# Matmul operands padded to lie alike mod 256 bytes, x loaded in quarters, and ten early pairs in a hybrid attention and MLP block

## The chip, the cores and the metric

The kernel runs on one core of a Trainium2 chip. The metric is the device time of one execution in microseconds (us). The time before is the median of three runs, 1524.86 us (1524.47 to 1524.96). A measurement of this kernel can tell a difference of about 0.2%, some 3 us, from no change.

Engines are named as in the profile: PE is TensorE's matmul, PEld its weight load, DVE is VectorE, ACT is ScalarE, POOL is GpSimd, SP is SyncE, which issues the DMAs.

## What is computed

One decoder layer on 1024 tokens of width 1024, in float32:

```python
h = rmsnorm(x, g_mix)
proj = h @ w_in            # q, k, v of three branches, an indexer, 3 gate groups
o_swa = sliding_window_attention(...)      # window 128, sinks
o_dsa = dsa_attention(...)                 # indexer scores, top 256 keys
o_mem = memory_cross_attention(...)        # 256 memory tokens
gates = sigmoid(gate_logits + b_gate)
merged = g0 * (o_swa @ w_proj_swa) + g1 * (o_dsa @ w_proj_dsa) + g2 * (o_mem @ w_proj_mem)
x = x + merged @ w_out
h = rmsnorm(x, g_mlp)
hid = square(relu(h @ w_mlp_in))           # 1024 x 4096
x = x + hid @ w_mlp_out
return rmsnorm(x, g_final)
```

## The kernel before, in words

Every large product is made of three matmuls of fp32r parts: each operand is split into a high part (a rounded copy, by ACT, line 93) and a low part (the rest, a subtraction on DVE or POOL), and `mm3` (lines 146 to 149) issues high x high, high x low and low x high into one PSUM bank. A matmul has a moving operand of up to 512 columns and a stationary operand of 128 columns, which a weight load brings in first. In a row of the profile the moving operand and the stationary one stand behind the arrow.

The stages, in the order of time:

- **Attention** (to 613 us). x is normalised and transposed, the indexer scores are computed, VectorE and ScalarE search the top 256 keys bit by bit (lines 535 to 575), and the three attention branches run. The gate products (`gt_g`, 24 units of 48 matmuls of 512 columns) have a low priority and fill PE between them.
- **Projections and merge** (613 to 745 us), with the gates read back from DRAM, then the **output projection** (`out_part`, line 908; tiles `mb_o`). It runs over `tg` (token halves) and `n` (column halves), and in each over `kp` (four pieces of w_out, 512 KB each, `raw_wo`). Each piece feeds 24 matmuls. Its result is added to x (line 982), which is loaded by eight DMAs of 512 KB (line 938) into the buffer `x2`. That buffer held `part` until then, so the DMAs wait for the last reader of `part` (line 905), and every DMA that stands behind them on SP's queue waits too.
- **Normalisation for the MLP** (to 890 us). Each token tile is scaled, transposed (`tb_h`, line 1003) and split. For the second token half the seven-product scheme of Strassen and Winograd needs sums of blocks (`T1` to `T4`, lines 1016 to 1024). While that runs, PE has the **early pairs**: for the first EARLY of 16 column pairs the two products that need the first token half alone (`mb_ep`, `mb_eq`, lines 1036 to 1047; 24 matmuls a pair). Their sum is squared behind a relu on DVE (line 1044), and both are written to DRAM.
- **MLP up** (`up_pair`, lines 1083 to 1119; 890 to 1158 us). A pair costs five products of 12 matmuls, and two more if it is not an early one. Weights are added on POOL (`load_pair`, lines 1073 to 1076) and split on ACT and DVE (`up_unit`).
- **MLP down** (`mb_dn`, lines 1135 to 1194; from 1158 us) and the final norm.

The order of the instructions on each engine is set ahead of time by a scheduler, by the priorities of `band`. Where a tile lies in SBUF is set by the pools: `base` at the bottom, `A2` above it (later `X2`, `C` and `X3` in its place), and from the other end `bigA` with the transposed activations (`hT`, `oT`, `h2T`), `A`, `G` and later `M` and `E`. The weights of most stages lie in `base` (`load_unit`, lines 112 to 122) or in `X3`. In the MLP's up stage `up_unit` goes round four slots, two in `base`, one in `X3`, one in `M`:

```python
i = ring["n"] % 4
(pool, tag, bufs) = ((base, "st", 2), (base, "st", 2), (X3, "w3", 1), (M, "u4", 1))[i]
```

## Time and profile before

| what | value |
|---|---|
| median of three runs | 1524.86 us |
| the profiled execution's own time | 1524.89 us |
| its span, first to last instruction | 1523.2 us |
| PE busy | 1454.0 us (95%) |
| DVE, ACT, POOL busy | 991.5, 638.5, 562.2 us |
| mean granted TensorE clock | 0.988 |
| DMA, mean | 106 GB/s |
| chain that ended last: PE, DVE | 71%, 17% |

The span is 1.7 us shorter than the execution's own time; what lies around it stays. Matmuls are pipelined: a row's duration holds the time in the pipeline too, and what a matmul costs in a dense stretch is the distance from its start to the next one's start. The idle time that stands before a row is the engine's own, and the arrow names what ended it.

### The profile page before, as it was taken

Reading aid. Unit: us, or ns where it says so; the run is one execution under the profiler, and the core shown is the slowest. Engines: PE = TensorE matmul, PEld = TensorE weight load, DVE = VectorE, ACT = ScalarE, POOL = GpSimd, SP = SyncE. Lnnn points to the kernel's source line nnn. Section 1 sums busy time; section 2 is a strip of 40 time slices with the busy share of each in tenths; the row PEclk is TensorE's granted clock in tenths of the full one; section 3 lists DMA queues with packets and bytes.
Section 4 is the critical chain, followed back from the end, with each engine's and each line's share of the span. In section 5 each row is a group of like instructions: output and inputs, shape, how many; then the busy total and the mean of one; then the engine's idle time right before and its main releaser. Section 6 shows DMA issues by size and latency. Waiting matters only on the chain.

```text
span 1523.2 us, 19743 instructions
## 1 busy us (share of the span) xinstructions
PE 1454.0 (95%) x7010; PEld 1215.7 (80%) x7010; DVE 991.5 (65%) x1909; ACT 638.5 (42%) x1251; POOL 562.2 (37%) x468
## 2 busy tenths in 40 slices
PE   6999999998899999999899989999998999999997
PEld 5888877897788988788678768888886888888886
DVE  7667999999986665757543966565555533444436
ACT  5545767875465444645345522222223220122213
POOL 4332224326567433445244753432223321222302
PEclk9999999999999999999999999999999999999999
DMA  6212331212112133546532444433326413323002
GB/s 215 84 56 84 104 90 58 74 46 69 50 35 70 42 100 102 158 129 215 195 131 89 146 139 142 152 127 115 101 96 230 155 59 111 111 111 111 28 14 97
DMA packets 133015, 161.51 MB, mean 106 GB/s; under 512 B 11284, under 2 KB 97332, under 8 KB 129844
## 3 DMA queue, kind: packets, MB, share of 16 engines
q1 hardware_dynamic: 132916, 160.25, 32.2%
q8 instruction: 55, 0.90, 0.3%
q14 instruction: 44, 0.36, 0.1%
HBM read 120.38 MB, written 39.85 MB: 105 GB/s over the span
## 4 chain that ended last, share of the span: by engine, by line
PE 71%; DVE 17%; issue 4%; DMA 3%; ACT 2%; POOL 1%; SPq 1%; DVEq 0%; ACTq 0%; POOLq 0%
PE mb_dn L148 7%; PE mb_dn L149 7%; PE mb_dn L147 7%; PE mb_u L147 5%; PE mb_u L148 5%; PE mb_u L149 5%; PE mb_o L919 4%; PE gt_g L148 4%; PE gt_g L147 4%; PE gt_g L149 4%; DVE tk_jk L538 3%; PE gt_p L148 1%; PE gt_p L147 1%; PE gt_p L149 1%; PE tb_u L148 1%
## 5 line engine op out<-in xcount | busy, mean ns | idle before, releaser
L148 PE MATMUL mb_dn<-wlo,hhi 128*128 128x512 f32 (+1 forms) x516 | 200.1, 388 | 1.2 <-POOL wlo L969 1.1
L147 PE MATMUL mb_dn<-whi,hhi 128*128 128x512 f32 (+1 forms) x516 | 197.9, 388 | 3.5 <-ACT whi L93 2.4
L149 PE MATMUL mb_dn<-whi,hlo 128*128 128x512 f32 (+1 forms) x516 | 200.0, 388 | 1.1 <-DVE hlo L969 1.1
L1168 DVE TENSOR_TENSOR x<-x,mb_dn 128x512 f32<-128x512 f32 x129 | 87.0, 681 | 167.8 <-PE mb_dn L149 166.9
L969 POOL TENSOR_TENSOR wlo<-wr,whi 128x1024 fp32r<-128x1024 f32 x32 | 84.9, 2670 | 225.4 <-ACT whi L93 220.2
L147 PE MATMUL gt_g<-hT_hi,hi_g 128*128 128x512 f32 x384 | 153.6, 400 | 2.0 <-DVE gs L825 1.6
L148 PE MATMUL gt_g<-hT_lo,hi_g 128*128 128x512 f32 x384 | 153.9, 401 | 0.0
L149 PE MATMUL gt_g<-hT_hi,lo_g 128*128 128x512 f32 x384 | 153.5, 400 | 0.0
L147 PEld LDWEIGHTS mb_dn<-whi,hhi 128*128 128x128 f32 x516 | 96.8, 188 | 24.1 <-ACT whi L93 2.8
L148 PEld LDWEIGHTS mb_dn<-wlo,hhi 128*128 128x128 f32 x516 | 96.9, 188 | 21.9 <-POOL wlo L969 2.1
L149 PEld LDWEIGHTS mb_dn<-whi,hlo 128*128 128x128 f32 x516 | 96.9, 188 | 21.1 <-DVE hlo L969 1.6
L93 ACT ACTIVATE hi_s<-r 128x1024 fp32r<-128x1024 f32 (+1 forms) x48 | 43.5, 916 | 165.0 <-PE mb_u L148 66.4
L93 ACT ACTIVATE hhi<-hr 128x1024 fp32r<-128x1024 f32 x32 | 32.7, 1048 | 180.8 <-PE mb_dn L148 158.6
L538 DVE TENSOR_SCALAR_CACHE_REDUCE tk_jk<-isc,tk_c 128x384 bf16<-128x384 f32 (+3 forms) x128 | 103.5, 808 | 2.5
L106 POOL TENSOR_TENSOR lo_g<-raw_g,hi_g 128x1024 fp32r<-128x1024 f32 x24 | 58.3, 2428 | 97.1 <-ACT hi_g L93 76.1
L147 PEld LDWEIGHTS gt_g<-hT_hi,hi_g 128*128 128x128 f32 x384 | 72.7, 189 | 18.2 <-DVE gs L825 2.0
L535 ACT ACTIVATE tk_jk<-isc,tk_c 128x1024 bf16<-128x1024 f32 x64 | 73.6, 1149 | 29.0 <-DVE tk_c L547 26.2
L149 PEld LDWEIGHTS gt_g<-hT_hi,lo_g 128*128 128x128 f32 x384 | 72.8, 189 | 14.8
L148 PEld LDWEIGHTS gt_g<-hT_lo,hi_g 128*128 128x128 f32 x384 | 72.6, 189 | 14.8
L147 PE MATMUL mb_u<-T_hi,hi_s 128*128 128x512 f32 x192 | 76.7, 399 | 7.0 <-ACT hi_s L93 7.0
L1073 POOL TENSOR_TENSOR r<-r,r 128x512 f32<-128x512 f32 x16 | 20.9, 1304 | 159.6 <-DMA r<-in_w_mlp_in_dram 159.6
L148 PE MATMUL mb_u<-T_lo,hi_s 128*128 128x512 f32 x192 | 76.8, 400 | 0.0
(452 smaller groups left out, 3907.5 us busy)
## 6 DMA issues: line engine op xcount, KB each, us to landing
wr<-in_w_mlp_out_dram SPq DMA_DIRECT2D x32, 512.0 KB, 3.5
hr<-hid_d SPq DMA_DIRECT2D x16, 1024.0 KB, 6.1
raw_g<-in_w_in_dram SPq DMA_DIRECT2D x24, 512.0 KB, 3.9
g_d<-gs SPq DMA_DIRECT2D x48, 256.0 KB, 2.0
gl<-g_d SPq DMA_DIRECT2D x48, 256.0 KB, 3.5
raw_wo<-in_w_out_dram SPq DMA_DIRECT2D x16, 512.0 KB, 3.5
r<-in_w_mlp_in_dram SPq DMA_DIRECT2D x16, 512.0 KB, 4.3
r<-in_w_mlp_in_dram SPq DMA_DIRECT2D x32, 256.0 KB, 2.9
```

Of the source, the lines that this page charges most:

```text
L93: nc.scalar.activation(o, i, AF.Copy)
L106: lo_engine.tensor_tensor(lo, raw, hi.bitcast(F32), op=ALU.subtract)
L147: nc.tensor.matmul(ps, st_hi, mv_hi, start=first, stop=False)
L148: nc.tensor.matmul(ps, st_hi, mv_lo, start=False, stop=False)
L149: nc.tensor.matmul(ps, st_lo, mv_hi, start=False, stop=last)
L535: nc.scalar.activation(jk[:, :n], isc[t], AF.Sign, bias=cand_f[:, j:j + 1], scale=-1.0, accum_out=cnt[:, j:j + 1])
L538: nc.vector.tensor_scalar(jk[:, :n], isc[t], cand_f[:, j:j + 1], 0.0, op0=ALU.is_ge, op1=ALU.add, accum_out=cnt[:, j:j + 1])
L919: nc.tensor.matmul(banks[i], st, (hi, hi, lo)[part_][:, kk_], start=(k == 0 and part_ == 0), stop=(k == KT - 1 and part_ == 2))
L969: engine.tensor_tensor(lo, raw, hi.bitcast(F32), op=ALU.subtract)
L1073: add(r2[:, lo4], r3[:, lo4], r2[:, hi4])
L1168: nc.vector.tensor_tensor(x2[:, t, cs], x2[:, t, cs], ps, op=ALU.add)
```

## The change

Four things. **Padding**: a pad of 96 bytes is put into `base` and one of 64 bytes into `A2`, `split_load` rounds the last dimension of its tiles up to 64 elements, and some small tiles are moved or resized, so that tiles start elsewhere. **x in quarters**: `load_x` loads 4 tiles of 512 columns (four DMAs of 256 KB) for one (tg, n) at a time. **EARLY** goes from 8 to 10. **Early stage**: the relu and square of an early pair go from one DVE operation to two ACT operations, and the low parts of the early pairs' weights and of `T3` go from POOL to DVE.

```diff
--- before.py
+++ after.py
@@ -34,7 +34,7 @@
 NEG_BIG = -float(2.0 ** 117)
 POS_BIG = float(2.0 ** 117)
 DSA_AHEAD = 2
-EARLY = 8
+EARLY = 10
 MERGE_WITH = (range(4), range(4, 6), range(6, 8), ())
 GATE_ORDER = [*range(8), *range(16, 24), *range(8, 16)]
 GATES_EARLY = 10
@@ -86,6 +86,9 @@
     p1_d = [dram.tile([P, 512], F32, name=f"p1_d{i}") for i in range(EARLY)]
 
     base = ctx.enter_context(tc.tile_pool(name="base", bufs=1))
+
+
+    base.tile([P, 24], F32, name="pad")
     ident_r = base.tile([P, P], F32R, name="ident")
     ident = ident_r.bitcast(F32)
 
@@ -98,7 +101,8 @@
         return hi, lo
 
     def split_load(slots, shape, srcs, nm, lo_engine):
-        raw, hi, lo = (pool.tile(list(shape), dt, tag=tag, name=f"{part}_{nm}", bufs=bufs)
+        pitch = list(shape[:-1]) + [-(-shape[-1] // 64) * 64]
+        raw, hi, lo = (pool.tile(pitch, dt, tag=tag, name=f"{part}_{nm}", bufs=bufs)[..., :shape[-1]]
                        for (pool, tag, bufs), dt, part in zip(slots, (F32, F32R, F32R), ("raw", "hi", "lo")))
         for (sl, src) in srcs:
             nc.sync.dma_start(raw if sl is None else raw[sl], src)
@@ -227,6 +231,7 @@
             chunk.append((hi, lo))
         return chunk
 
+    A2.tile([P, 16], F32, name="pad2")
     ident_f = A2.tile([P, P], F32, tag="rl", name="ident_f", bufs=2)
     make_identity(nc, ident_f)
     act_copy(ident_r, ident_f)
@@ -249,7 +254,7 @@
     sink8 = A2.tile([P, 8], F32, name="sink8")
     nc.sync.dma_start(sink8, sinks[0].partition_broadcast(P))
     nc.vector.tensor_scalar(sink8, sink8, 8.0, None, op0=ALU.mult)
-    invf = A2.tile([P, 32], F32, name="invf")
+    invf = A.tile([P, 32], F32, tag="o_sb", name="invf", bufs=2)
     nc.sync.dma_start(invf, inv_freq.partition_broadcast(P))
     pos_i = p_tile([P, P], "pos_i", I32)[:NT]
     nc.sync.dma_start(pos_i, positions[0].rearrange("(t p) -> t p", p=P))
@@ -262,8 +267,8 @@
     nc.tensor.transpose(tpc[:, 32:56], bg_r, ident[:24, :24])
     pos = A2.tile([P, NT], F32, name="pos")
     nc.vector.tensor_copy(pos, tpc[:, 0:NT])
-    bgate = A.tile([P, 24], F32, name="bgate")
-    nc.vector.tensor_copy(bgate, tpc[:, 32:56])
+    bgate = A.tile([P, 32], F32, name="bgate")
+    nc.vector.tensor_copy(bgate[:, :24], tpc[:, 32:56])
 
 
     cur_ok = A2.tile([P, P], I32, name="cur_ok")
@@ -557,8 +562,8 @@
             eqb = A2.tile([P, S], BF16, tag="rl", name=f"{gn}_eq{t}", bufs=2)[:, :n]
             cum = A2.tile([P, S], F32, tag="cum", name=f"{gn}_cum{t}")[:, :n]
             if on_act:
-                mn = A2.tile([P, 1], F32, tag="tk_mn", name=f"{gn}_mn{t}", bufs=2)
-                up = A2.tile([P, 1], I32, tag="tk_up", name=f"{gn}_up{t}", bufs=2)
+                mn = A2.tile([P, 1], F32, tag="tk_mn", name=f"{gn}_mn{t}")
+                up = A2.tile([P, 1], I32, tag="tk_up", name=f"{gn}_up{t}")
                 nc.vector.tensor_scalar(le, isc[t], T, 0.0, op0=ALU.is_le, op1=ALU.add, accum_out=c1)
                 nc.vector.scalar_tensor_tensor(cum, le, F32_MAX, isc[t], op0=ALU.mult, op1=ALU.add)
                 nc.gpsimd.affine_select(out=cum[:, t * P:], in_=cum[:, t * P:], pattern=[[-1, n - t * P]],
@@ -922,20 +927,25 @@
 
     for d in range(KT):
         merge_unit(0, d)
+
+    def load_x(tg, n):
+        with band("w"):
+            for t in range(4 * tg, 4 * tg + 4):
+                nc.sync.dma_start(x2[:, t, n * 512:(n + 1) * 512], x[t * P:(t + 1) * P, n * 512:(n + 1) * 512])
+
     first_banks = [mb_bank(f"o00{i}") for i in range(4)]
     for kp in range(KT // 2):
         out_part(0, 0, first_banks, kp)
         for d in MERGE_WITH[kp]:
             merge_unit(1, d)
+        if kp == 2:
+            x2 = X2.tile([P, NT, D], F32, tag="x2", name="x2")
+            load_x(0, 0)
 
     ctxC.close()
     X3 = ctx.enter_context(tc.tile_pool(name="X3", bufs=1, reuse_waits="tile"))
     late["pool"], late["n"] = X3, 0
 
-    x2 = X2.tile([P, NT, D], F32, tag="x2", name="x2")
-    with band("w"):
-        for t in range(NT):
-            nc.sync.dma_start(x2[:, t], x[t * P:(t + 1) * P, :])
 
 
 
@@ -970,11 +980,13 @@
 
     ctxM = ExitStack()
     for tg in range(2):
-        ss = X3.tile([P, 2, 4], F32, tag="n_ss4", name=f"ss2_{tg}", bufs=2)
+        ss = X3.tile([P, 2, 16], F32, tag="n_ss4", name=f"ss2_{tg}", bufs=2)[:, :, :4]
         for n in range(2):
             cs = slice(n * 512, (n + 1) * 512)
             banks = [mb_bank(f"o{tg}{n}{i}") for i in range(4)] if tg or n else first_banks
             for kp in range(KT // 2 if tg or n else 0):
+                if kp == 2:
+                    load_x(tg, n)
                 out_part(tg, n, banks, kp)
             with band("crit"):
                 for i in range(4):
@@ -1020,7 +1032,7 @@
                     nc.vector.scalar_tensor_tensor(lo, tps[1], -1.0, hi.bitcast(F32), op0=ALU.mult, op1=ALU.subtract)
                     nc.vector.scalar_tensor_tensor(t3, tps[1], -1.0, t3, op0=ALU.mult, op1=ALU.add)
                     nc.vector.tensor_tensor(t4, t4, t2, op=ALU.subtract)
-                    for dst, src, e in ((T2, t2, nc.vector), (T3, t3, nc.gpsimd), (T4, t4, nc.gpsimd), (T1, t1, nc.vector)):
+                    for dst, src, e in ((T2, t2, nc.vector), (T3, t3, nc.vector), (T4, t4, nc.gpsimd), (T1, t1, nc.vector)):
                         split(*(v[:, :, ts] for v in dst), src, e)
 
     def product(ps, w, mv):
@@ -1034,14 +1046,15 @@
 
 
     for c in range(EARLY):
-        a11, a12 = halves(load_unit(wcol[2 * c], f"wi{2 * c}", nc.gpsimd))
+        a11, a12 = halves(load_unit(wcol[2 * c], f"wi{2 * c}", nc.vector))
         ps1, ps2 = mb_bank(f"ep{c}"), mb_bank(f"eq{c}")
         st = M.tile([P, 2, 512], F32, tag=("stg", "u4_lo")[c % 2], name=f"st{c}")
         product(ps1, a11, B11)
         act_copy(st[:, 0], ps1)
         product(ps2, a12, B21)
         nc.vector.tensor_tensor(st[:, 1], ps2, st[:, 0], op=ALU.add)
-        nc.vector.scalar_tensor_tensor(st[:, 1], st[:, 1], 0.0, st[:, 1], op0=ALU.max, op1=ALU.mult)
+        nc.scalar.activation(st[:, 1], st[:, 1], AF.Relu)
+        nc.scalar.activation(st[:, 1], st[:, 1], AF.Square)
         with band("w"):
             nc.sync.dma_start(p1_d[c], st[:, 0])
             nc.sync.dma_start(hid_d[c][:, 0], st[:, 1])
```

Byte address, mod 256, at which a matmul's moving and stationary operand start, in the built programs (matmuls of 512 columns, unless another width is given):

| products | matmuls | before: moving, stationary | changed |
|---|---|---|---|
| gates `gt_g` | 1152 | 224, 128 | 224, 224 |
| projections `gt_p`, `mm_p`, `mb_p`, `tb_p` | 384 | 224, 128 | 224, 224 |
| memory queries `mm_mq` | 96 | 224, 64 | 224, 224 |
| output projection `mb_o` | 384 | 128 or 192, 224 | 224, 224 |
| early pairs `mb_ep`, `mb_eq` | 192 (240 in the changed one) | 224, 128 or 192 | 224, 224 |
| MLP up, weights in `base` or `X3` | 720 | 224, 128 or 192 | 224, 224 |
| MLP up, weights in `M` | 432 | 224, 224 | 224, 224 |
| MLP down `mb_dn` | 1524 | 224, 224 | 224, 224 |
| attention scores `sc_` | most | 32, 32 | 32, 32 |
| projections of 384 columns (`mm_s`, `mm_dp`) | 576 | 64, 224 | 224, 224 |

So 2928 matmuls of 512 columns lie unlike before and alike in the changed kernel (1152 + 384 + 96 + 384 + 192 + 720). Transposes and the products with the probabilities stay unlike.

Up to the output projection the order on every engine is the same in both programs. The first place where it moves is SP's queue at the load of x (`x` is the tile x2, `raw_wo` a piece of w_out). Before:

```order
L104 DMA raw_wo_8099<-in_w_out_dram 128x2x512
L938 DMA x_8067<-in_x_dram 128x1024 x8
L104 DMA raw_wo_8129<-in_w_out_dram 128x2x512
L104 DMA raw_wo_8159<-in_w_out_dram 128x2x512
L958 DMA g_mlp_t<-in_g_mlp_dram 128x1024
L104 DMA raw_wo_8189<-in_w_out_dram 128x2x512
```

Changed:

```order
L108 DMA raw_wo_8099<-in_w_out_dram 128x2x512
L934 DMA x_8037<-in_x_dram 128x512 x4
L108 DMA raw_wo_8129<-in_w_out_dram 128x2x512
L934 DMA x_8037<-in_x_dram 128x512 x4
L108 DMA raw_wo_8163<-in_w_out_dram 128x2x512
L934 DMA x_8037<-in_x_dram 128x512 x7
L108 DMA raw_wo_8193<-in_w_out_dram 128x2x512
L934 DMA x_8037<-in_x_dram 128x512
```

One piece of w_out stood behind 4 MB of x and now stands behind 1 MB of it; the later ones have 1 MB, 1.75 MB and 0.25 MB more of x ahead of them.

The second place is POOL during the normalisation (`xn` a token tile, `lo_wi` the low part of an early pair's weights, `T_lo` the low part of T3 or T4, `r_0` the first weights of the up stage). Before:

```order
L965 TENSOR_TENSOR xn_8659<-xn_8659,g_mlp_t 128x512
L106 TENSOR_TENSOR lo_wi_8862<-raw_wi_8860,hi_wi_8861 128x1024
L106 TENSOR_TENSOR lo_wi_8900<-raw_wi_8898,hi_wi_8899 128x1024
L969 TENSOR_TENSOR T_lo<-xn_8630,T_hi 128x4x128
L106 TENSOR_TENSOR lo_wi_8938<-raw_wi_8936,hi_wi_8937 128x1024
L969 TENSOR_TENSOR T_lo<-braw_8079,T_hi 128x4x128
L965 TENSOR_TENSOR xn_8688<-xn_8688,g_mlp_t 128x512
L106 TENSOR_TENSOR lo_wi_8976<-raw_wi_8974,hi_wi_8975 128x1024
```

Changed:

```order
L975 TENSOR_TENSOR xn_8671<-xn_8671,g_mlp_t 128x512
L979 TENSOR_TENSOR T_lo<-braw_8079,T_hi 128x4x128
L975 TENSOR_TENSOR xn_8700<-xn_8700,g_mlp_t 128x512
L979 TENSOR_TENSOR T_lo<-braw_8079,T_hi 128x4x128
L975 TENSOR_TENSOR xn_8729<-xn_8729,g_mlp_t 128x512
L979 TENSOR_TENSOR T_lo<-braw_8079,T_hi 128x4x128
L1086 TENSOR_TENSOR r_0_9150<-r_0_9151,r_0_9150 128x512
```

All ten `lo_wi` and the four low parts of T3 are gone from POOL.

The third place is DVE at the end of the normalisation, up to the first result of the up stage (`st` the products of an early pair, `lo_s` the low part of the up stage's first weights). Before:

```order
L969 TENSOR_TENSOR h2T_lo<-braw_8078,h2T_hi 128x4x128
L1022 TENSOR_TENSOR braw_8079<-braw_8079,xn_8717 128x4x128
L1043 TENSOR_TENSOR st_8982<-mb_eq_8981,st_8982 128x512
L969 TENSOR_TENSOR T_lo<-xn_8717,T_hi 128x4x128
L1044 SCALAR_TENSOR_TENSOR st_8982<-st_8982 128x512
L1043 TENSOR_TENSOR st_9020<-mb_eq_9019,st_9020 128x512
L1044 SCALAR_TENSOR_TENSOR st_9020<-st_9020 128x512
L969 TENSOR_TENSOR lo_s_0_9062<-r_0_9051,hi_s_0_9061 128x1024
```

Changed:

```order
L1055 TENSOR_TENSOR st_9000<-mb_eq_8999,st_9000 128x512
L1034 TENSOR_TENSOR braw_8079<-braw_8079,xn_8729 128x4x128
L110 TENSOR_TENSOR lo_wi_9111<-raw_wi_9109,hi_wi_9110 128x1024
L979 TENSOR_TENSOR h2T_lo<-braw_8078,h2T_hi 128x4x128
L979 TENSOR_TENSOR T_lo<-xn_8729,T_hi 128x4x128 x2
L1055 TENSOR_TENSOR st_9039<-mb_eq_9038,st_9039 128x512
L979 TENSOR_TENSOR lo_s_0_9160<-r_0_9149,hi_s_0_9159 128x1024
L1055 TENSOR_TENSOR st_9078<-mb_eq_9077,st_9078 128x512
L979 TENSOR_TENSOR lo_s_0_9168<-r_0_9151,hi_s_0_9167 128x512
L1055 TENSOR_TENSOR st_9117<-mb_eq_9116,st_9117 128x512
```

The squares (L1044) are gone from DVE, and two more sums of early pairs stand among the low parts of the up stage's weights. On PE, 39 matmuls of early pairs stood between the last transpose of a token tile and the first product of the up stage; now 81 do.

## Rows read from the trace of the kernel before

**Rows 1.** Windows by stage: us, busy of each engine (instructions), PEclk, DMA share, GB/s.

```profile
141.00:415.00 274.00, 260.14 (x1387) 223.14 (x1386) 265.95 (x676) 189.84 (x432) 105.86 (x118) 0.99 0.24 70
...
745.00:831.00 86.00, 77.77 (x341) 62.36 (x340) 32.49 (x48) 36.99 (x66) 32.05 (x16) 0.94 0.43 147
831.00:890.00 59.00, 49.31 (x225) 39.19 (x225) 51.97 (x64) 28.85 (x47) 41.29 (x22) 0.97 0.47 143
890.00:1158.00 268.00, 268.00 (x1153) 217.27 (x1152) 155.99 (x198) 57.45 (x66) 86.03 (x62) 0.99 0.37 124
```

**Rows 2.** Waits of PE over the span: us in total, times, longest.

```profile
PE mb_o L919 <- ACT hi_wo L93: 9.1, 2, 8.2
PE mb_u L147 <- ACT hi_s L93: 7.0, 1, 7.0
```

**Rows 3.** Timeline of PE, first matmuls of successive products of 12: pair 6, pair 7.

```profile
980.00 0.39 PE L147 MATMUL mb_u<-T_hi,hi_s 128*128 128x512 f32 x1
...
982.80 0.39 PE L147 MATMUL tb_u<-h2T_hi,hi_s 128*128 128x512 f32 x1
...
993.96 0.39 PE L147 MATMUL mb_u<-T_hi,hi_s 128*128 128x512 f32 x1
...
996.68 0.39 PE L147 MATMUL tb_u<-h2T_hi,hi_s 128*128 128x512 f32 x1
```

**Rows 4.** PE groups by form: count, busy us, mean ns, idle before.

```profile
L147 PE MATMUL mb_dn<-whi,hhi 128*128 128x512 f32 x508 | 195.6, 390 | 3.5 <-ACT whi L93 2.4 <-DVE hid L1113 1.1
L147 PE MATMUL gt_g<-hT_hi,hi_g 128*128 128x512 f32 x384 | 153.6, 400 | 2.0 <-DVE gs L825 1.6 <-ACT gs L823 0.4
L355 PE MATMUL sc_Sd<-kT_d,qT_dp 128*128 128x512 f32 x24 | 9.8, 410 | 0.0
```

**Rows 5.** Window 141 to 415, instructions on the gates' tile alone (columns as above, without POOL).

```profile
141.00:415.00 274.00, 134.78 (x536) 100.10 (x535) 9.66 (x13) 6.77 (x10) 0.99 0.24 70
```

**Rows 6.** Timeline of SP (start, us, line), then of PE.

```profile
747.40 3.78 SPq L938 DMA_DIRECT2D x<-in_x_dram  x8
751.29 1.44 SPq L104 DMA_DIRECT2D raw_wo<-in_w_out_dram  x2
...
763.17 0.80 PE L919 MATMUL mb_o<-hi_wo,mg_hi 128*128 128x512 f32 x1 [8.23 <-ACT hi_wo L93]
...
767.58 0.40 PE L919 MATMUL mb_o<-hi_wo,mg_hi 128*128 128x512 f32 x1
```

**Rows 7.** Chain of waits through that stall: start, us, what.

```profile
751.29 10.69 DMA raw_wo<-in_w_out_dram
...
762.06 1.06 ACT hi_wo L93
```

**Rows 8.** Groups of DVE, POOL and ACT in 831 to 889; low parts on DVE (ns, min/median/max).

```profile
L1044 DVE SCALAR_TENSOR_TENSOR st<-st 128x512 f32<-128x512 f32 x8 | 13.0, 1627 | 0.1
...
L969 DVE TENSOR_TENSOR T_lo<-xn,T_hi 128x512 fp32r<-128x512 f32 x4 | 5.4, 1355 | 0.0
...
L106 POOL TENSOR_TENSOR lo_wi<-raw_wi,hi_wi 128x1024 fp32r<-128x1024 f32 x6 | 15.3, 2551 | 6.1 <-ACT hi_wi L93 6.1
...
L93 ACT ACTIVATE T_hi<-xn 128x512 fp32r<-128x512 f32 x8 | 5.0, 628 | 2.8 <-DVE xn L1019 1.9 <-DVE xn L1021 0.8
...
L106 DVE TENSOR_TENSOR lo_wo<-raw_wo,hi_wo x8: 1216/1226/2295, 704.0 to 769.0; 128x1024 fp32r<-128x1024 f32 x8
```

**Rows 9.** Chain of waits into the up stage: start, us, what.

```profile
887.80 1.07 ACT hi_s L93
...
888.91 0.79 PE mb_u L147
889.70 0.43 PE mb_u L148
...
893.97 0.24 PE mb_u L149
```

**Rows 10.** Timeline of PE, the last transposes of the normalisation.

```profile
872.12 0.63 PE L1003 MATMUL tb_h<-ident,xn 128*128 128x128 f32 x4 [1.13 <-DVE xn L1021]
```

## The prediction
> **What bounds the kernel now.** I read the windows by stage first, since the engines' shares over the span mix stages with different limits. They show PE as the bound nearly everywhere: in the MLP's up stage for 268.00 of 268 us [rows 1]. Three stretches differ. From 141 to 415 us VectorE is busy for 265.95 of 274 us and PE waits for it. From 745 to 831 PE is busy for 77.77 of 86 us, and from 831 to 890 for 49.31 of 59 [rows 1]. The waits of PE put names to the last two: 9.1 us for a piece of w_out, one of them 8.2 us, and 7.0 us for the first weights of the up stage [rows 2]. So there is time to win in two ways: in the cost of a matmul where PE is full, and in the two holes.
>
> **The padding.** In a dense stretch a matmul costs the distance between starts. The timeline of the up stage has the same work from two places. The third product of pair 6 takes its weights from `base`, where the stationary operand starts at 128 and the moving one at 224: 12 matmuls from 980.00 to 982.80, 233 ns each. The third product of pair 7 takes them from `M`, where both start at 224: 12 matmuls from 993.96 to 996.68, 227 ns each [rows 3]. The difference is 6.6 ns (2.80 less 2.72 us, over 12). The mean durations go the same way: 400 ns for the gates, which lie unlike, 390 ns for the MLP's down stage, which lies alike [rows 4]. What the rows cannot part is the address from the place: `M` and the down stage's pool are at the end of SBUF that `base` is not. I take the address as the cause, because the change moves no pool and its padding is then worth the whole difference; the other reading is a rival.
>
> 2928 matmuls go from unlike to alike. Of these, those that lie under VectorE's stretch win nothing, since the end of that stretch is VectorE's: 536 gate matmuls [rows 5] and the 96 memory queries, 632 in all. The 192 of the early pairs I count below. That leaves 2104 matmuls by 6.6 ns, **13.9 us**. The bounds are nothing (the place is the cause) and 18.1 us (2736 matmuls, where VectorE's stretch shortens too). I stay at the measured difference without the covered ones. The 576 matmuls of 384 columns have no row of the same width in both layouts that is as dense; I set them at nothing, with at most 6.6 ns each, 3.8 us, as the other bound.
>
> The trace speaks against a rule here. The Trainium skill (SBUF — State Buffer, section Who interferes with whom) gives PE two read ports of SBUF, one for the moving operand and one for the weight load, independent of each other, and says that PE never waits on anyone. By it the two addresses could not matter, this term would be zero, and the sum below 15 us smaller. The trace has a difference between two equal products [rows 3], so it does not agree, unless the place makes it.
>
> The other edits of this part (a wider pitch, small tiles moved, one buffer for two in the select) add no operation and leave the order on all engines as it was up to the output projection. The buffer that is gone makes a tile's minimum wait for the tile before it, and both stand in order on VectorE anyway. I set them at nothing.
>
> **x in quarters.** SP issues x at 747.40, when the last reader of `part` is done, and the piece of w_out that PE needs next at 751.29, behind 4 MB [rows 6]. It takes 10.69 us to land, then ACT splits it in 1.06 us and PE starts at 763.17, after 8.23 us of nothing [rows 6, 7]. The idle costs more than itself: the next ten matmuls, to 767.58, stand 0.44 us apart [rows 6], against 0.23 [rows 3]: after the idle time the granted clock is at the lower of its two levels, 1.2 GHz, and it is 0.94 over the stage [rows 1]. Ten by 0.21 is 2.1 us. In the changed order 1 MB stands ahead of that piece. 4.5 MB took from 747.40 to the landing at 761.98, 14.6 us, or some 320 bytes per ns with the latency in it; so 1.5 MB take about 5 us, the piece lands near 752.5, and with ACT's 1.06 us PE could have it at about 753.5. PE ran dry at 754.94. The stall goes. What is late next are the pieces behind: the one after the batch of seven has 5.25 MB ahead of and including itself, 17 us, so it is there at 764.4 and split at 765.5; PE wants it two pieces of 24 matmuls after 754.9, at 765.8. That is close, and I set 1.5 us against the gain. The term is 8.2 + 2.1 - 1.5 = **8.8 us**, with bounds of 4 (a second hole of 5 us, below) and 10.3.
>
> **The early stage.** PE's hole of 7.0 us before the up stage [rows 2] ends with a chain from POOL's sums through ACT's split to PE at 888.91 [rows 9]. From there to 893.97 the chain has eleven matmuls, all but the first 0.43 us apart [rows 9]: 5.06 us in place of 2.6, of which I put 2.3 down to the lower clock and the rest to the first one's way through the pipeline. The two added pairs put 48 matmuls, 11 us of PE's work, into the normalisation, and take the same 48 out of the up stage. So PE's sum is unchanged, and the hole is filled where the chain is not later: 81 matmuls, 18.4 us, now follow the last transpose, where the whole way from the last transposes, at 872.12 [rows 10], to the up stage's first product took 16.8 us. I take both, 9.3 us.
>
> This holds only if the others keep pace. VectorE was busy for 51.97 of 59 us [rows 1]. It loses eight squares, 13.0 us, and gains eight low parts of weights inside the stretch, at 1.23 us each by the rows for the same shape on VectorE, 9.8 us; four low parts of T3, half as large and so set at half of that, 2.5 us; and two sums of the same size, 1.2 us [rows 8]. That is 0.5 us more. The dear end is 2.3 us for a low part (its longest row) and 1.36 for one of T3, 25 us with the sums, 12 more than the squares [rows 8]. I take the cheap end, because the operations that got dear stood beside POOL's, and POOL loses 15.3 us of `lo_wi` in the stretch and four operations of T3 [rows 8]. ACT gains two operations a pair; the nearest row is a split of the same size, 0.63 us [rows 8], so 20 of them are 12.6 us on 28.85 of 59: covered, and if ACT were the bound the cost would be a few us at most. The added DMAs (two weights of 512 KB, two stores and loads) meet a queue that is busy for 0.47 of the time [rows 1]; PE's work hides them. The 192 old early matmuls win 1.3 us by the padding, and I give 0.5 back for waits that stay. The term is 9.3 + 1.3 - 0.5 = **10.1 us**, with bounds of nothing and 13.
>
> **The sum.** 13.9 + 8.8 + 10.1 = 32.8 us, off the profiled execution's own time of 1524.89 us, which is the median within 0.03 us: **1492 us**.
>
> **Rivals.**
> - *The place, not the address, sets a matmul's cost.* The padding is worth nothing and the other terms stay: 1492 + 13.9 + 1.3 = 1507 us. For it: the fast products [rows 3, 4] have their weights at one end of SBUF. Against it: the attention scores, with both operands at that end, are no faster than the gates (410 against 400 ns, [rows 4]). The rule on PE's ports in the Trainium skill (SBUF — State Buffer) would give the same time. 8%.
> - *VectorE becomes the bound of the early stage.* At the dear end it has 64 us of work where PE has 240 matmuls, 54.5 us at 227 ns, and the transposes, and its in-order queue holds the low parts that PE waits for. The stall before the up stage stays in another form, and the term falls to nothing: 1502 us. For it: VectorE is the fullest engine after PE there. Against it: the sum of its work hardly changes at the cheap end. 10%.
> - *The batch of seven makes a new hole.* If 256 KB pieces move more slowly than the 512 KB ones, the piece behind it comes 5 us late, with up to 2 us of lower clock: 1498 us. 12%.
> - *Slower: alike operands collide.* The alike rows of the scores are 10 ns longer than the unlike ones of the gates [rows 4]; if that is what likeness does, and the pools at the far end are fast for another reason, the 2296 matmuls (2104 and 192) cost 10 ns more each, 23 us, against 17.6 us won elsewhere (8.8, and 10.1 less 1.3): 1524.9 + 5.4 = 1530 us. It decides from 7.7 ns on. Against it: the two pairs [rows 3], and that the scores are short groups that wait on other engines. 4%.
> - *No change at all*, where a new wait eats every term: 1525 us. 1%.
>
> **The numbers.** My forecast has 65%. From 1481 (VectorE's stretch, the 384-column matmuls and the remaining waits all give something, 11 us) to 1507 the range holds it and the first three rivals, 95% by these cases; as the terms were each taken from one row, I leave it there and count it as 8 in 10. A change is told from none at 0.2%, 3 us. Faster: the forecast and the first three rivals, 95%, of which I take one off for what I have not seen: 94%. Same 2%, slower 4%.
>
> **What would show it.** The padding: starts 227 ns apart in gates, output projection and all pairs of the up stage, and mean durations near 390 ns; the up stage some 18 us shorter (48 matmuls fewer, 672 at 6.6 ns less, no slow start). x: no wait over 2 us for `hi_wo` and a granted clock near 1.00 from 745 to 831. The early stage: no wait for the first `hi_s`, its length about as before, VectorE's operations there nearer to their short rows. I am wrong if unlike places stay at 233 ns though alike, if a wait of over 4 us for `hi_wo` or for an early pair's low part appears, or if VectorE's stretch in the attention moves.

## The result and the profile after

The changed kernel takes **1501.02 us** (median of 4 runs, 1495.05 to 1501.37) against 1524.66 us of the kernel before on the same chip: a ratio of 0.984 (95% interval 0.981 to 0.987), some 23.6 us less. The forecast was 1492 us with a range of 1481 to 1507. So direction and range hold, and 9 of the 33 us forecast did not come. The profiled execution took 1501.37 us, with a span of 1499.7 us; PE is busy for 1441.7 us (96%).

The windows by stage of the changed kernel, cut where the stages now end (columns as in [rows 1]):

```profile
139.00:413.00 274.00, 259.08 (x1384) 224.45 (x1383) 265.49 (x674) 189.74 (x432) 106.66 (x118) 0.98 0.24 70
...
741.00:818.50 77.50, 74.48 (x345) 61.59 (x344) 34.38 (x51) 36.56 (x65) 28.96 (x14) 1.00 0.49 163
818.50:876.50 58.00, 58.00 (x273) 48.07 (x272) 46.97 (x70) 40.92 (x68) 18.27 (x12) 1.00 0.56 171
876.50:1132.50 256.00, 253.55 (x1106) 207.82 (x1106) 150.24 (x192) 57.18 (x67) 85.52 (x62) 0.99 0.40 132
1132.50:1499.00 366.50, 351.94 (x1548) 290.28 (x1547) 168.35 (x261) 77.20 (x102) 92.47 (x41) 0.98 0.28 101
```

VectorE's stretch is 274 us long as before. The second line answers to 745 to 831 of [rows 1]: 77.5 us in place of 86, and the clock is at 1.00. The early stage is full now, 58.00 of 58 us with 48 instructions more on PE. The up stage takes 256 us where it took 268 [rows 1], but PE is not busy in all of it any more.

The waits of PE in the changed kernel (us in total, times, longest) answer to [rows 2]. `hi_wo` is the high part of a piece of w_out, `hi_s` and `lo_s` are the high and low parts of the up stage's weights, `whi` is the high part of the down stage's:

```profile
PE mb_o L924 <- ACT hi_wo L96: 3.9, 2, 3.0
PE mb_dn L151 <- ACT whi L96: 3.2, 1, 3.2
...
PE mb_u L151 <- ACT hi_s L96: 2.1, 1, 2.1
```

The 8.2 us for w_out are now 3.0. The 7.0 us for `hi_s` at the up stage's start are gone; the 2.1 us are another wait, 70 us into the stage. Before, PE waited 2.4 us for `whi`.

Now the padding. The timeline of PE shows the third product of a pair again, as [rows 3] did, first with weights in `M` (pair 5), then with weights in `base` (pair 6):

```profile
954.29 0.39 PE L151 MATMUL mb_u<-T_hi,hi_s 128*128 128x512 f32 x1
...
957.01 0.39 PE L151 MATMUL tb_u<-h2T_hi,hi_s 128*128 128x512 f32 x1
...
967.89 0.39 PE L151 MATMUL mb_u<-T_hi,hi_s 128*128 128x512 f32 x1
...
970.61 0.39 PE L151 MATMUL tb_u<-h2T_hi,hi_s 128*128 128x512 f32 x1
```

Both take 2.72 us for 12 matmuls, 227 ns each. In [rows 3] the product from `base` took 2.80. The groups by form (count, busy us, mean ns, idle before) answer to [rows 4]:

```profile
L151 PE MATMUL mb_dn<-whi,hhi 128*128 128x512 f32 x508 | 196.9, 392 | 4.4 <-ACT whi L96 3.2 <-DVE hid L1126 1.3
L151 PE MATMUL gt_g<-hT_hi,hi_g 128*128 128x512 f32 x384 | 153.4, 400 | 1.8 <-DVE gs L830 1.8
...
L924 PE MATMUL mb_o<-lo_wo,mg_hi 128*128 128x512 f32 x128 | 36.8, 390 | 0.0
```

The gates' mean is still 400 ns, though their starts have moved closer: over all dense starts (under 300 ns, no wait between) of the gates the mean distance falls from 234.2 to 229.9 ns, of the output projection from 233.8 to 227.1, of `mb_u` from 231.4 to 227.0. A mean duration was the wrong row to look for this in. The gates gain least because they run in short bits between other products: the first eight dense starts behind a gap or a narrower matmul are still 232.0 ns apart on average (235.0 before), the later ones 227.6 (233.5 before).

**Where the 23.5 us between the two profiled executions lie**, by the starts of the stages: 2.9 in the attention (1.9 of them in the first loads: PE waited 10.3 us there in the kernel before and 8.3 to 8.5 in all other profiled runs, padded or not, so these are not the change's), 1.1 in the projections, 8.0 in the output projection, 13.4 in the early and up stages, and the down stage is 1.9 longer. The forecast had 4.1, 2.5, 11.3, 14.9 and 0. Two places explain most of what is missing. First, the wait in the up stage; the chain of waits into it (start, us, what), then the timeline of PE behind it:

```profile
935.41 0.61 DVE lo_s L979
...
936.04 4.83 DMA r<-in_w_mlp_in_dram
...
941.03 1.29 POOL r L1086
...
943.53 2.28 POOL r L1087
...
945.84 1.07 ACT hi_s L96
```

```profile
946.95 0.50 PE L151 MATMUL mb_u<-T_hi,hi_s 128*128 128x512 f32 x1 [2.07 <-ACT hi_s L96]
...
948.87 0.63 PE L151 MATMUL mb_u<-T_hi,hi_s 128*128 128x512 f32 x1
949.30 0.63 PE L152 MATMUL mb_u<-T_lo,hi_s 128*128 128x512 f32 x1
```

`r3` has one buffer. It comes free when the low part of the pair before is done, at 936.02; then its load, POOL's sums and ACT's split follow one another, and PE has the weights at 946.9. PE finished the last product of pair 3 at 931.1, which started this turn of the loop: 15.8 us, where a pair now costs PE 13.6. Behind the wait the starts are 0.43 us apart, the lower of the two levels of the clock (1.2 GHz): 2.1 us of wait and some 2 of slow matmuls. The same stands at the start of the down stage: 3.2 us of wait, then twelve slow matmuls from 1146.80 on (granted clock 0.50), 2.7 us.

Second, w_out. The timeline of ACT (start, us), then of PE:

```profile
752.30 0.63 ACT L996 ACTIVATE jk<-x 128x512 bf16<-128x512 f32 x1 [2.06 <-DVE x L994]
...
753.06 0.63 ACT L996 ACTIVATE jk<-x 128x512 bf16<-128x512 f32 x1
...
753.69 1.04 ACT L96 ACTIVATE hi_wo<-raw_wo 128x1024 fp32r<-128x1024 f32 x1
```

```profile
754.78 0.50 PE L924 MATMUL mb_o<-hi_wo,mg_hi 128*128 128x512 f32 x1 [3.02 <-ACT hi_wo L96]
755.12 0.39 PE L924 MATMUL mb_o<-hi_wo,mg_lo 128*128 128x512 f32 x1
755.35 0.40 PE L924 MATMUL mb_o<-hi_wo,mg_hi 128*128 128x512 f32 x1
```

ACT's split of the piece that PE waits for stands behind squares of x + merged w_out, the last two of which waited for x itself. But PE does not wait for the squares. The piece was issued behind 1 MB of x and landed 6.7 us later, at 753.5, and the split began 0.2 us after that. The timeline of SP, then the time from the piece's issue to its landing:

```profile
744.94 1.76 SPq L934 DMA_DIRECT2D x<-in_x_dram  x4
746.80 0.38 SPq L108 DMA_DIRECT2D raw_wo<-in_w_out_dram  x1
...
DMA to landing us min/median/max: 6.7/6.7/6.7
```

Behind this wait the starts stay 0.23 apart: not every wait of 3 us is followed by slow matmuls.

### The profile page after: what moved, and what is told of

It reads as the page before. It is cut to its first block, busy times and chain, and to the rows that moved or that the text cites. A ratio compares the mean times of both kernels' runs of the same rounds, so it can differ in the third digit from the quotient of the medians.

```text
span 1499.7 us, 19772 instructions
## 1 busy us (share of the span) xinstructions
PE 1441.7 (96%) x7010; PEld 1216.6 (81%) x7010; DVE 977.4 (65%) x1911; ACT 649.2 (43%) x1271; POOL 535.1 (36%) x456
## 4 chain that ended last, share of the span: by engine, by line
PE 63%; DVE 19%; issue 6%; DMA 5%; POOL 3%; ACT 3%; SPq 0%; POOLq 0%; DVEq 0%; ACTq 0%
PE mb_dn L151 8%; PE mb_dn L152 8%; PE mb_dn L153 8%; PE mb_o L924 4%; PE gt_g L151 4%; PE gt_g L152 4%; PE gt_g L153 4%; DVE tk_jk L543 3%; DMA r<-in_w_mlp_in_dram 2%; PE mb_u L151 2%; PE mb_u L153 2%; PE mb_u L152 2%; POOL r L1087 1%; PE gt_p L152 1%; PE gt_p L151 1%
## 5 line engine op out<-in xcount | busy, mean ns | idle before, releaser
L979 POOL TENSOR_TENSOR wlo<-wr,whi 128x1024 fp32r<-128x1024 f32 x32 | 84.6, 2658 | 227.0 <-ACT whi L96 221.8
L979 DVE TENSOR_TENSOR lo_s<-r,hi_s 128x1024 fp32r<-128x1024 f32 (+1 forms) x48 | 51.1, 1070 | 56.8 <-ACT hi_s L96 51.1
```

Of the source, the lines that this page charges most:

```text
L979: engine.tensor_tensor(lo, raw, hi.bitcast(F32), op=ALU.subtract)
```

## Experiments

Each time is a median; the kernel before ran beside them at 1522.8 to 1523.4 us.

**One part at a time, and the change without its pad.** The first three are the kernel before with the hunks of the diff for one part each (padding; `load_x`; EARLY with the moved squares and low parts). The fourth is the changed kernel with one line less:

```diff
-    base.tile([P, 24], F32, name="pad")
```

`pad_only`: 

> The kernel before with the padding edits alone. If the address mod 256 sets a matmul's cost (theory), matmuls in the gates, the output projection and the up stage start about 227 ns apart as in the changed kernel, where they were 231 to 234 ns apart; by the dense means of the two traces that is 2.6 us in the gates behind VectorE's stretch, 1.8 in the projections, 2.6 in the output projection, 1.1 in the early pairs and 5.1 in the up stage, 13 us: about 1511.5 us, with the 8.2 us stall for w_out and the 7.0 us one before the up stage still there. If the place sets it (rival), starts stay where they were and the time is 1524.7 us. If the saving is given back in waits (second rival), the starts are 227 ns apart and the time falls by less than 8 us.

Measured: 1511.41 us (ratio 0.992, 0.991 to 0.994). The starts fell to 229.8 ns in the gates, 228.1 in the output projection and 226.9 in `mb_u`, with every operand of a matmul in the pool it had before. So the place is not the cause and the address is. The 8.1 us for w_out and 6.1 for the first `hi_s` stand. The up stage has its 1152 matmuls and no wait worth naming after its start:

```profile
877.10:1141.40 264.30, 263.89 (x1153) 217.47 (x1154) 157.53 (x198) 58.38 (x67) 85.51 (x63) 0.99 0.38 126
```

`x_only`: 

> The kernel before with x loaded in quarters and nothing else. The prediction's term was 8.8 us: 1516 us, with no wait for w_out over 2 us. The changed kernel shows a wait of 3.0 us there, which came behind four squares on ScalarE (theory: that wait belongs to this edit and not to the faster matmuls): then 8.2 us go to about 3, the 2.1 us at the lower clock go too, and the time is about 1517.5 us. Rival: in the kernel before PE runs dry 3 us later, so the piece is in time and the wait is under 1 us, 1514.5 us.

Measured: 1517.36 us (0.996, 0.994 to 0.997), a gain of 5.5 us. PE waited 2.4 us for w_out, with seven slow matmuls (1.5 us) behind it. The piece was issued at 749.93 and landed 6.7 us later, at 756.6; ACT split it from 756.76 on. So the wait belongs to this edit, and the prediction's 1.5 us for what stays was too small by 2.4.

`early_only`: 

> The kernel before with ten early pairs and the moved squares and low parts, no padding, old load of x. The prediction's term without its padding part was 8.8 us: 1516 us, with no wait for the first hi_s. Theory after the result: the hole of 7.0 us and its 2.3 us at the lower clock go, and no new wait comes in the up stage, because a pair there takes 13.9 us with unlike operands and the weights of a pair take about 15 us in a loop that only the faster matmuls outrun: 1515.5 us. Rival: the two more early pairs alone use up the lead of the weights, a wait of 2 us and its low clock stand in the up stage here too, 1520 us.

Measured: 1512.58 us (0.993, 0.992 to 0.994), a gain of 10.2 us, more than either account. The up stage has no wait at all:

```profile
889.75:1145.30 255.55, 255.55 (x1106) 207.25 (x1105) 151.18 (x191) 56.16 (x64) 85.77 (x62) 1.00 0.40 130
```

`nopad`: 

> The changed kernel without the pad of 96 bytes in base alone, so that the weights in base and X3 lie at 128 again (the moving or stationary partner at 224), everything else as changed. Theory (address): starts go back to 232 to 234 ns, 13 us more, 1514 us; if the wait of 2.1 us in the up stage with its slow matmuls (4.4 us in all) is there only because the matmuls are faster, it goes and the time is 1510 us. Rival (place): 1501 us.

Measured: 1504.28 us (0.988, 0.986 to 0.989). The starts go back to 234.2 ns in the gates and 231.8 in `mb_u`, yet the time rises by only 3.3 us against the changed kernel's median (5.8 by the ratios, each to the kernel before on its own chip). Both accounts by the address (1514 and 1510 us) are too high. The whole padding, of which this line moves the weights in `base` and `X3`, was worth 11.4 us alone. By the starts of the stages the profiled execution is 4.8 us longer than the changed kernel's up to the output projection and 1.4 in the early stage, but 0.2 shorter in the output projection, where PE waits 1.4 us for w_out and not 3.0, equal in the up stage, and 2.2 shorter in the down stage, where PE waits 2.0 us for `whi` and no slow matmuls follow. The up stage:

```profile
882.40:1138.30 255.90, 255.90 (x1106) 207.30 (x1105) 151.59 (x191) 56.17 (x64) 86.13 (x62) 1.00 0.39 130
```

255.9 us without a wait and at full clock, against 256 us with matmuls that are 2% cheaper: with ten early pairs the stage takes the same time either way.

**Address or place, in the stage that was fast.** The weights' slots of the down stage are moved against each other by 32 bytes a slot; pool and work stay.

```diff
-E.tile([P, D], F32R, tag=f"{par}{nm}_{part_}", ...)
+E.tile([P, D + (8 if nm == "w" else 0)], F32R, tag=f"{par}{nm}_{part_}", ...)[:, :D]
```

`dn_spread`: 

> The changed kernel with the weight tiles of the down stage 32 bytes wider, so that their slots start elsewhere mod 256 while pool, order and work stay. The stationary operand stays at 224; the moving one lies 0, 32, 64, 96 bytes (mod 256) behind it for the four high parts (254 matmuls each) and 128, 160, 192, 224 behind it for the four low parts (127 each). If the address sets the cost (theory), only the 254 matmuls at distance 0 stay 227 ns apart and the other 1270 go to 231 to 234 ns: 5 to 9 us more, about 1508 us, and the four distances 32 to 224 show whether the cost depends on the distance. If the place sets it (rival), all stay at 227 ns and the time is 1501 us.

Measured: 1503.31 us (1500.11 to 1507.24; 0.986, 0.984 to 0.988), so in the total it is barely told from the changed kernel. The stage tells it. The same 200 us of the down stage, here and in the changed kernel:

```profile
1200.00:1400.00 200.00, 200.00 (x867) 162.41 (x866) 79.57 (x88) 31.72 (x32) 43.29 (x17) 1.00 0.24 89
```

```profile
1200.00:1400.00 200.00, 200.00 (x884) 165.66 (x883) 80.08 (x89) 31.70 (x32) 43.11 (x17) 1.00 0.25 89
```

867 matmuls in place of 884, at full clock and with PE never idle: 230.7 ns in place of 226.2. The mean distance of starts by the distance of a matmul's own operands is 229.7 ns at 0, 231.3 at 32, 232.8 at 64 and 96, 233.0 at 128, 232.1 at 160, 227.3 at 192 and 228.1 at 224. So the address acts here too, but the prediction's rule is too simple: alike operands among unlike neighbours cost 229.7 and not 226.7, and the moving operand 192 bytes on is nearly free. What the neighbours' addresses do was not taken apart. A further 256 bytes between the two starts changes nothing: at each distance both halves of the matmuls, told apart mod 512, agree within 0.5 ns.

**What the early stage needs.** The kernel before with the count alone, and with the other hunks of the early stage alone:

```diff
-EARLY = 8
+EARLY = 10
```

`early_count`: 

> The kernel before with ten early pairs in place of eight and nothing else. The prediction filled the hole of 7.0 us and its 2.3 us at the lower clock by the two more pairs, and counted the moved squares and low parts as 0.5 us of VectorE: then nearly all of the 10.2 us that ten pairs and moved engines gave together comes here, 1514 us. Rival: POOL, with ten low parts of weights and those of T3 before its sums for the up stage, makes the sums later by two low parts (5.1 us), and half of the hole stays: 1518 us.

Measured: 1521.67 us (0.999, 0.998 to 1.000). Both accounts fall: the two pairs alone bring 1.7 us. The profiled execution, 1518.10 us, was the shortest of twelve, so its rows can be kinder than the median. The window of its early stage, the squares among VectorE's groups there, and what PE waited for:

```profile
829.80:893.80 64.00, 61.22 (x272) 48.97 (x271) 55.62 (x67) 31.55 (x52) 46.99 (x24) 0.97 0.52 158
```

```profile
L1044 DVE SCALAR_TENSOR_TENSOR st<-st 128x512 f32<-128x512 f32 x9 | 16.2, 1795 | 0.2
```

```profile
871.50 0.63 PE L1003 MATMUL tb_h<-ident,xn 128*128 128x128 f32 x4 [2.42 <-DVE xn L1021]
```

The stage takes 64 us where `early_only` took 59.35 with the same matmuls. The hole at the up stage's start is filled, but VectorE, with 55.62 us of work and squares of 1795 ns, hands the token tiles to PE's transposes late, and the lower clock follows. VectorE did become the bound, in the half of the change that did not relieve it.

`early_engines`: 

> The kernel before with the squares on ScalarE and the low parts of the early weights and of T3 on VectorE, eight early pairs as before. By the prediction the two pairs fill the hole and the engines only keep pace: a gain of 0 to 3 us, 1520 to 1523 us. Rival: POOL, freed of eight low parts and four of T3, makes the first sums of the up stage earlier and takes most of the hole away by itself: 1516 us or less.

Measured: 1519.61 us (0.997, 0.996 to 0.998), 3.7 us, a little over the first account. The first `hi_s` is there 5 us earlier (883.74), but only 39 matmuls cover the way to it, and 4.8 us of the hole stay. Together the two edits bring 10.2 us, apart 1.7 and 3.7: the pairs fill a hole only if VectorE and POOL keep pace, and the engines' relief is worth something only if there is work to fill the hole.

**Taking the new waits away.** `s4_pool` (changed kernel):

```diff
-        split(hi, lo, raw[:, cols], nc.vector)
+        split(hi, lo, raw[:, cols], nc.vector if n == KT else nc.gpsimd)
```

> The changed kernel with the low part of the up stage's last operand (lo_s of 512 columns, one a pair) on POOL and not on VectorE. In the changed kernel the loop that ends at the wait of 2.1 us goes: last product of pair 3 done at 931.1, ScalarE's split, then lo_s on VectorE behind four operations on hid until 936.02, which frees r3, its load of 4.83 us, POOL's sums, ScalarE's split, PE at 946.9. Theory: this loop of 15.8 us against 13.6 us of PE's work a pair is what the faster matmuls outrun; with lo_s done by about 933 it is 3 us shorter, the wait and its slow matmuls (4.4 us) go, and the time is about 1497 us. Rival: POOL is late instead (1.3 us more of work a pair before its next sums, or the loop is set by another buffer), the wait stays: 1501 us.

Measured: 1499.75 us (1496.72 to 1501.24; 0.984, 0.982 to 0.986), not told from the changed kernel. The wait at the sixth pair is gone and three others, 3.3 us in all, came later. The chain into one of them goes over another link: `r3` was free at 1001.7, and its load stood on SP's queue behind the store of `hid`, which waited for VectorE until 1004.11.

```profile
1004.12 0.34 SPq L1132
...
1004.57 4.32 DMA r<-in_w_mlp_in_dram
```

`jk_late` (changed kernel): the four squares of the first column half are written behind the second piece of w_out of the next one.

```diff
                 out_part(tg, n, banks, kp)
+                if kp == 1 and n:
+                    squares(tg, 0, ss)
...
-                    jk = X3.tile([P, 512], BF16, tag="junk", name=f"jk2_{t}{n}")
-                    nc.scalar.activation(jk, x2[:, t, cs], AF.Square, accum_out=ss[:, n, i:i + 1])
+                if n:
+                    squares(tg, n, ss)
```

> The changed kernel with the four squares of the first half of x + merged w_out (two quarters of x2) written behind the second piece of w_out of the next column half. In the changed kernel ScalarE's split of the piece that PE waits for (3.0 us, until 754.78) stood behind four squares, and the last two of these waited for x until 752.30. Theory: the piece itself landed before that, so the wait falls by the time of those squares, to under 1.5 us: 1499 us. Rival: the piece lands at about 753.5, as 1 MB of x stands ahead of it, and the wait hardly changes: 1501 us.

Measured: 1495.70 us (1491.73 to 1497.11; 0.981, 0.979 to 0.983), the lowest of all. Its reason is not the one given. The scheduler left all four squares ahead of the split, so the edit did not do what it was made for. The split waits for the piece itself, as the rival says and as it did in the changed kernel, and PE still waits 2.0 us:

```profile
751.50 1.06 ACT L96 ACTIVATE hi_wo<-raw_wo 128x1024 fp32r<-128x1024 f32 x1 [0.19 <-DMA raw_wo<-in_w_out_dram]
```

By the starts of the stages the profiled execution is 1.1 us shorter than the changed kernel's up to the output projection, 1.0 in it, 0.9 in the up stage, where the waits fell to 1.5 us in pieces of at most 0.6 with no slow matmuls behind them, and 2.7 in the down stage, whose waits fell from 5.6 to 3.7 us. No edit stands in the last two; what moved them was not taken apart.

`fix3` (both edits and a third, where the down stage loads its first `hid`):

```diff
-            raw = X3.tile([P, 4, 512], F32, tag="braw", name=f"hr{c}{q}", bufs=2)
...
+            if c == 0 and q == 1:
+                raws = [X3.tile([P, 2, 512], F32, tag="xn", name=f"hr01{i}", bufs=2) for i in range(2)]
```

> The two edits before together, and a third: the second block of hid that the down stage reads first goes into the two buffers of the up stage's weight sums (free once the last pair's weights are split) instead of the buffer of the last pair's result, so that its load is not issued behind that pair's store (1137.87 in the changed kernel, and PE waited 3.2 us until 1146.80 and ran twelve matmuls at the lower clock, 2.7 us). Theory: the three waits and their slow matmuls (3.0, 4.4 and 5.9 us) are what was given back of the padding's gain; without them the time is 1488 to 1491 us, and the granted clock is 0.99 or more. Rival: others come in their place (the loop of the weights a few pairs later, the low part of the weights in the down stage), and it is above 1496 us.

Measured: 1500.43 us (0.985, 0.983 to 0.986). The rival's account holds. The up stage waits 4.2 us, no less than with `s4_pool` alone, and w_out 2.7 us, this time with slow matmuls behind it.

`r3_two` (changed kernel):

```diff
-        r3 = X3.tile([P, KT, P], F32, tag="gvec", name=f"r3_{c}")
+        r3 = (X3, M)[c % 2].tile([P, KT, P], F32, tag=("gvec", "stg")[c % 2], name=f"r3_{c}")
```

> The changed kernel with two buffers in place of one for the operand r3 of the up stage's sums (the second is the buffer stg, free once the early pairs are stored). Theory: the up stage takes 256.0 us, whether its matmuls cost 227 ns (changed kernel) or 231.5 (ten early pairs without padding: 255.6), because the one buffer r3 makes a loop of 14 to 16 us a pair; with two, the loads run a pair ahead, no wait for hi_s is left in the up stage, and it takes 1104 times 226.9 ns and the pipeline's end, 251 to 252 us: 4 to 5 us less than the changed kernel, 1496.5 us. Rival: another buffer of the ring (ud, xn, w3) sets the loop, and waits of 2 us or more for hi_s stay: 1500 to 1501 us.

Measured: 1496.56 us (1494.22 to 1501.21; 0.983, 0.981 to 0.984). The window of its up stage, then all of PE's waits there:

```profile
875.50:1129.30 253.80, 251.52 (x1105) 206.83 (x1104) 155.03 (x191) 54.99 (x64) 84.27 (x62) 1.00 0.40 131
```

```profile
PE mb_u L153 <- DVE lo_s L979: 2.1, 2, 1.8
```

No wait for `hi_s` is left, the clock is at 1.00, and PE's busy time is the 251.5 us expected. What is late next is a low part on VectorE, 2.1 us, so that the stage takes 253.8 us and not 251 to 252. So the loop through `r3` was the cause of the wait in the changed kernel. That the median came out as forecast is in part luck: of the 5.2 us between the two profiled executions 1.9 lie in the up stage, and 2.2 in the down stage, which the edit does not touch.

`jk_hr_r3` (`r3_two`, `jk_late` and the block of `hid`): 

> The changed kernel with r3 in two buffers, the late squares, and the second block of hid in the free buffers of the weight sums; the low part on VectorE as it was. Theory: each takes its own wait with the slow matmuls behind it (late squares 4 to 5 us, r3 4 to 5, hid 3 to 5): 1487 to 1490 us, clock 0.99 or more. Rival: waits and the lower clock behind them come and go by small shifts, so that the sum is not reached: 1493 to 1497 us.

Measured: 1501.23 us (1497.25 to 1502.21; 0.984, 0.983 to 0.986): the rival's side, and above even its range. In this order the buffer `stg` comes free late, by the store of the last early pair that used it; the chain into a wait of 1.5 us at 892.3, which slow matmuls follow:

```profile
878.42 4.89 DMA hid_d<-st
...
883.36 2.86 DMA r<-in_w_mlp_in_dram
```

No version is shown to be faster than the changed kernel: the intervals of `jk_late` and `r3_two` overlap with its own (0.981 to 0.987), though their medians are 4 to 5 us lower.

## Why the prediction was right, and where it was off

The sum was 32.8 us; 23.6 came. The parts alone gave 11.4 + 5.5 + 10.2 = 27.1 us. So 5.7 us were lost in the sizes of the terms, and 3.5 us between them.

- **The padding, 13.9 us and 1.3 in the early pairs: 11.4 alone.** The mechanism holds, and the place as the cause falls (`pad_only`). Addresses alone made the starts 4 to 7 ns closer. The Trainium skill (SBUF — State Buffer, section Who interferes with whom) calls PE's read ports for the moving operand and for the weight load independent; these runs do not agree with two operands that cannot disturb each other. The 6.6 ns were right for the output projection (6.7) and for those products of the up stage that lay unlike, but not for the gates, which gained 4.3: 616 matmuls outside VectorE's stretch by 2.3 ns is 1.4 us. The 6.6 came from a long dense run, and the gates' bits are short. The 384-column matmuls, set at nothing, came 1 to 2 ns closer (181 to 179 or 180), some 0.4 us outside that stretch. By the distances of starts 13 us should have come; the last 2 are within the spread of the runs. That VectorE's stretch would not move was right (274 us in both).
- **x in quarters, 8.8 us: 5.5 alone.** The stall of 8.2 us went, as said, but 2.4 us took its place (3.0 in the changed kernel). The step that failed is "so 1.5 MB take about 5 us, the piece lands near 752.5". From the first issue of x to the landing of the piece it took 8.5 us in `x_only` (748.06 to 756.6) and 8.6 in the changed kernel (744.94 to 753.5). The 320 bytes per ns were a mean over 4.5 MB, and the beginning is slower: in the kernel before, the third DMA of x, which also makes 1.5 MB, landed at 754.2, 6.8 us after the first issue. Why the quarters took 1.7 us more than that was not taken apart. PE ran dry at 755.5 in `x_only`, near the 754.94 of the working, and at 751.8 in the changed kernel. ACT's squares, which stand ahead of the split, ended as the piece landed and cost at most 0.2 us. The batch of seven, which the 1.5 us were for, made no hole.
- **The early stage, 10.1 us with its padding: 10.2 alone without it.** The size is right and the reason is half right. "This holds only if the others keep pace" was the condition; the working took it as nearly met before the change (VectorE +0.5 us), and `early_count` shows that it was not. VectorE's work in the stage fell, from 51.97 of 59 us [rows 1] to 46.97 of 58, instead of rising. A low part of weights cost 1.53 us and not 1.23, but other operations that had stood beside POOL's became short, as the prediction had said in words and not in the sum. Which of them do so is not settled by POOL's low parts alone: in `early_count`, where POOL has all of them, the sum below took 682 ns and the squares 1795. VectorE's groups in the stage, first one of the kernel before, then two of the changed kernel (count, busy us, mean ns):

```profile
L1022 DVE TENSOR_TENSOR braw<-braw,xn 128x512 f32<-128x512 f32 x4 | 6.1, 1517 | 0.0
```

```profile
L110 DVE TENSOR_TENSOR lo_wi<-raw_wi,hi_wi 128x1024 fp32r<-128x1024 f32 x8 | 12.2, 1528 | 0.5 <-ACT hi_wi L96 0.4
...
L1034 DVE TENSOR_TENSOR braw<-braw,xn 128x512 f32<-128x512 f32 x4 | 2.7, 683 | 0.0
```

- **What no term held: supply.** The working asked of each stall what is late next, but not of the faster matmuls. In the up stage of the kernel before, PE needed 13.9 us a pair, and ACT had the weights of a pair ready every 14.2 us (third pair at 915.7, ninth at 1001.0). The lead of the weights, 6 us at the second pair, covered that and was down to 1 us at the ninth. At 13.6 us a pair the lead is used up at the sixth pair, and 2.1 us of wait and some 2 of slow matmuls come back: the stage became 12 us shorter [rows 1] and not the 18 that the working named as a sign. `nopad` and `r3_two` show it from both sides. The down stage is 1.9 us longer, with waits as long in sum as before but 2.7 us of slow matmuls behind one; moving its block of `hid` did not settle that.
- **The rivals.** Of the four mechanisms only VectorE's bound was seen, in `early_count`, without the relief. Alike operands do not collide. The fastest run of the changed kernel, 1495.05 us, has a mean clock of 0.995 where the others have 0.986 to 0.988: 6 of the 9 us missing against 1492 can come and go from run to run, and its clock points to slow matmuls; which waits that run lacked was not seen.

## What to carry to other kernels

Where matmuls run back to back, look at the distance of starts, not at durations, and compare products that differ in the addresses of their operands alone; 2 to 3% can lie there. Before counting a cheaper matmul as gain, divide the stage by its turns and set PE's new time per turn against the loop that brings its operands (buffer free, load, sum, split): where the loop is longer, the gain ends when the lead is used up, and a wait can bring slow matmuls with it. Before a transfer is counted from a mean rate, look at when the first megabyte of a batch landed. Try the parts of a change alone and the whole without each: here 1.7 and 3.7 us made 10.2 together, and 11.4 alone was worth 3 to 6 on top of the rest.

## What the runs showed of the hardware

- The distance of starts of a 512-column fp32r matmul depends on where its operands begin mod 256 bytes: 226.7 ns in the down stage, where all lie at 224, 233 to 234 at the mixtures of the kernel before (128 or 192 with 224), and 227.3 to 233.0 in `dn_spread`, with an order in the distances that has no simple rule. In the first eight matmuls of a run less of it is seen: 232.0 ns in the gates of the changed kernel, 235.0 in those of the kernel before.
- Slow matmuls follow some waits of PE and not others: in the changed kernel 0.43 us a start or more for seven after the wait of 2.07 us in the up stage and for twelve after 3.17 us in the down stage, none after 3.02 us in the output projection.
- VectorE's operations with both inputs in SBUF can stretch beside POOL's: a square of 512 columns took 1627 ns on average in the early stage before [rows 8] and 1795 in `early_count`, from 692 ns for the one with nothing of POOL's beside it to 2969. Not all do: the sums that read an early pair's product from PSUM took 676 to 692 ns beside POOL too, and the sum of `braw` and `xn` 682 ns in `early_count`.
- A batch of DMAs begins slower than its mean: in the kernel before, 1.5 MB were there 6.8 us after the first issue and 4.5 MB 14.6 us after it, issuing and latency included.
